# First stage of an encoder block: modulation weights transposed and summed along rows by VectorE, x transposed tile by tile, six column groups of w_in

## The chip, the cores and the metric

The kernel runs on one core of one Trainium2 chip. The metric is the device time of one execution in microseconds. The engines are TensorE (PE, and PEld for its weight loads), VectorE (DVE), ScalarE (ACT), GpSimd (POOL) and SyncE (SP), which issues nearly all DMA transfers here.

## What is computed

One layer of a transformer encoder on 512 tokens of width 2048, in float32. Only the parts around the change are kept here.

```python
c_act = silu(c)                                   # c: 1 x 2048
mod = c_act @ w_ada + b_ada                       # w_ada: 2048 x 12288
sh1, sc1, g1, sh2, sc2, g2 = split(mod, 6)        # 2048 values each
h = rms_norm(x, norm1_w) * (1 + sc1) + sh1        # x: 512 x 2048
proj = h @ w_in                                   # w_in: 2048 x 8704
qa, ka, va, qb, kb, vb, ga, gb = split(proj)      # 1024 256 256 1024 1024 1024 2048 2048
ya = global_attention(rope(norm(qa)), rope(norm(ka)), va)    # 8 heads, 2 k/v heads
yb = neighbourhood_attention(qb, kb, vb, bias)               # 8 heads
m = sigmoid(ga) * (ya @ w_oa) + sigmoid(gb) * (yb @ w_ob)
x = x + g1 * (m @ w_out)
h2 = rms_norm(x, norm2_w) * (1 + sc2) + sh2
x = x + g2 * ((silu(h2 @ w_gate) * (h2 @ w_up)) @ w_down)
out = rms_norm(x, final_w)
```

## The kernel before

Everything is tiled by 128: 16 k-tiles of the width (`KT`), four token tiles (`NT`). A matrix product is done in three matmuls (`mm3`, lines 122 to 124): each operand is split into a high part `hi`, a copy rounded to float32r by ScalarE (line 114), and a low part `lo`, the remainder, by VectorE or, where `eng=G` or `G` is given, GpSimd (line 115). `unit` loads a piece of a weight, at most 128x1024 (512 KB), into a `raw` buffer (4 of them), and `wsplit` splits it into `whi` and `wlo` (3 of each). `form2` makes 512 columns for all tokens (8 units of 24 matmuls of 128x512), `form1` 256 columns, transposed (4 units of 24). The first column groups of w_in are KA (256 columns of k and 256 of v), QA (first half of qA), QA + 512 (second half), VB and VB + 512 (halves of vB) and GA (gate columns 0 to 511).

The author's code states an order; a scheduler of the framework fixes at build time which instruction each engine and each DMA queue runs when, and where they wait. It goes by program order (`tc.high_priority()` puts a block ahead), by the readiness of inputs and by free buffers, so work of a later stage can be moved up to where an engine would be idle. On the chip each engine and each queue runs its list in that fixed order.

*First stage* (lines 299 to 396). x is loaded as 16 tiles of 128x512; squares and statistics give the row factor, line 325 scales the tiles, TensorE transposes all of them (line 328) and ScalarE copies them to `xnT`, which holds the whole of x transposed. For the shift and the scale of each k-tile `ada1` calls `ada_mod`: pieces of w_ada are loaded (line 242; rows of 512 bytes for one k-tile, 1 KB for two), VectorE multiplies each piece by its value of silu(c) and adds it to `acc` (lines 255 and 257), so that each of 16 parts leaves one partial sum per partition; TensorE sums over the partitions by matmuls with a column of ones (line 275), and lines 263 to 265 make `s` and `t`. The loop runs over nine slices (k-tile 0, k-tile 1, then pairs). In each, ScalarE makes `hf` from xnT (line 351) and the split gives h of that k-tile, with GpSimd for the low part; all w_in splits of the stage have GpSimd too. KA is summed in four banks over the whole stage (lines 359 to 364); QA and GA are done in batches of one to four k-tiles in other banks and added up in SBUF by VectorE (line 391). At the end GA goes to DRAM.

*Attention A.* k and q are normalised and rotated, four heads run, then `form2(w_in, QA + 512, ...)`, the gates of columns 512 to 1023, four more heads, the gates of columns 1024 to 2047.

*Attention B.* `bg` holds generators of background work; `pump`, called after each unit of `form1` and `form2`, advances the first of them by one step. Before attention B eight `ada_mod` for the second modulation (pairs of k-tiles, nine steps each) are put there. Each half of B makes v by `form2(w_in, VB + half * 512, ...)`, then q and k of two heads at a time by `form1` (32 units in all for both halves), then those heads. Then come the eight `ada_gate` (nine steps each) and the gates `sg_b` (32 units). Output projections and the feed-forward part follow; the change doesn't touch them.

Of the kernel before, what the change touches and what calls it, by code (L numbers as in the profile page):

```python
# [17 lines left out]
P = 128  # L18
D = 2048
# [61 lines left out]
def encoder_block(ctx: ExitStack, tc, xp, c, w_ada, b_ada, norm1_w, w_in, q_norm_w, k_norm_w, tb,  # L81
# [147 lines left out]
    t2 = const.tile([P, KT], F32, name="t2")  # L229

    accp = io

    def ada_units(cols, w, pool=None):

        nj = len(cols)
        nk = 1024 // (nj * w)
        for k0 in range(0, KT, nk):
            raw = (pool or wp).tile([P, 1024], F32, tag="raw", name="raw", bufs=5 if pool else wbufs["raw"])
            r4 = raw.rearrange("p (k c n) -> p k c n", k=nk, c=nj)
            for j, col in enumerate(cols):  # L240
                src = w_ada[k0 * P:(k0 + nk) * P, col:col + w]
                nc.sync.dma_start(r4[:, :, j], src.rearrange("(k p) n -> p k n", p=P))
            yield [(k0 + e, raw[:, e * nj * w:(e + 1) * nj * w]) for e in range(nk)]

    def ada_acc(cols, w, bias, pool=None):


        acc = accp.tile([P, 512], F32, tag="acc", name="acc", bufs=2)[:, :len(cols) * w]
        if bias:
            G.memset(acc, 0.0)  # L250
            nc.sync.dma_start(acc[0:1, :], b_ada[:, cols[0]:cols[0] + w])
        for parts in ada_units(cols, w, pool):
            for k, part in parts:
                if k == 0 and not bias:
                    V.tensor_scalar(acc, part, cact[:, k:k + 1], None, op0=ALU.mult)
                else:
                    V.scalar_tensor_tensor(acc, part, cact[:, k:k + 1], acc, op0=ALU.mult, op1=ALU.add)  # L257
            yield None
        yield acc

    def ada_done(y, k0, n, s, b_s, nw, t, b_t):
        sl = slice(k0, k0 + n)
        V.tensor_add(s[:, sl], y[:, :n], b_s[:, sl])
        V.tensor_add(t[:, sl], y[:, n:2 * n], b_t[:, sl])
        V.scalar_tensor_tensor(s[:, sl], s[:, sl], 1.0, nw[:, sl], op0=ALU.add, op1=ALU.mult)

    def ada_mod(sh, sc, k0, n, to, pool=None):

        for acc in ada_acc((sc + k0 * P, sh + k0 * P), n * P, False, pool):
            if acc is None:  # L270
                yield
        with tc.high_priority():
            y = bank("Y")
            for j in range(2 * n):
                nc.tensor.matmul(y[:, j:j + 1], acc[:, j * P:(j + 1) * P], ones[:, 0:1], start=True, stop=True)
            ada_done(y, k0, n, *to)
        yield

    def ada_gate(col, q, dst):

        for acc in ada_acc((col + q * 512,), 512, True):
            if acc is None:
                yield
# [8 lines left out]
        yield  # L292

    def rows(dst, src):
        for q in range(4):
            nc.sync.dma_start(dst[:, q * 512:(q + 1) * 512], src[q].partition_broadcast(P).rearrange("p o d -> p (o d)"))
# [3 lines left out]
    xt = [[p_h.tile([P, 512], F32, tag=f"h{15 - 2 * i - q // 2}{'hl'[q % 2]}", name=f"xt{i}{q}") for q in range(4)]  # L300
          for i in range(NT)]
# [5 lines left out]
    g_acc = [p_x.tile([P, T], F32, name=f"g_acc{j}") for j in range(4)]  # L307
# [22 lines left out]
    hT = [pair(p_h, f"h{k}", T, 1) for k in range(KT)]  # L330

    sg_a = [dram.tile([P, T], F32, name=f"sga{j}") for j in range(KT)]
    sg_b = [dram.tile([P, T], F32, name=f"sgb{j}") for j in range(KT)]
    kv_b = [bank("mm") for _ in range(NT)]
    turn = itertools.cycle("SST")
    slices = [(0, 1), (1, 2)] + [(k, k + 2) for k in range(2, KT, 2)]

    def ada1(k0, k1):  # L340
        to = (s1, b_sc1, n1, t1, b_sh1)
        for _ in ada_mod(0, D, k0, k1 - k0, to, p_x):
            pass

    ada1(*slices[0])
    for n, (k0, k1) in enumerate(slices):
        hp = tc.high_priority()
        hp.__enter__()
        for k in range(k0, k1):
            hf = io.tile([P, T], F32, tag="io", name="hf")  # L350
            S.activation(hf, xnT[:, k], AF.Identity, scale=s1[:, k:k + 1], bias=t1[:, k:k + 1])
            split(*hT[k], hf, G)
        hp.__exit__(None, None, None)
        ks = range(k0, k1)
        hi, lo = wsplit(w_in, k0, len(ks), KA, 512, G)
        for k in ks:
            for i in range(NT):
                sl = slice(i * P, (i + 1) * P)
                nc.tensor.matmul(kv_b[i], hT[k][0][:, sl], hi[:, k - k0], start=k == 0, stop=False)
                nc.tensor.matmul(kv_b[i], hT[k][0][:, sl], lo[:, k - k0], start=False, stop=False)  # L360
        for k in ks:
            for i in range(NT):
                sl = slice(i * P, (i + 1) * P)
                nc.tensor.matmul(kv_b[i], hT[k][1][:, sl], hi[:, k - k0], start=False, stop=k == KT - 1)
        if k1 == KT:
            kv = []
# [3 lines left out]
        for c0, accs, ends in ((QA, q_acc, (0, 1, 2, 4, 8, 12, 16)), (GA, g_acc, (0, 2, 6, 10, 14, 16))):  # L370
            if k1 not in ends:
                continue
            a0 = ends[ends.index(k1) - 1]
            ws = {}
            for k in range(a0, k1, 2):
                m = min(2, k1 - k)
                hi, lo = wsplit(w_in, k, m, c0, 512, G)
                ws.update({k + e: (hi[:, e], lo[:, e]) for e in range(m)})
            for i, acc in enumerate(accs):
                sl = slice(i * P, (i + 1) * P)  # L380
                b = bank(next(turn))
                for k in range(a0, k1):
                    (wh, wl), (hh, hl) = ws[k], hT[k]
                    if accs is q_acc:
                        mm3(b, hh[:, sl], hl[:, sl], wh, wl, k == a0, k == k1 - 1)
                    else:
                        mm3(b, wh[:, sl], wl[:, sl], hh, hl, k == a0, k == k1 - 1)
                if a0 == 0:
                    S.activation(acc, b, AF.Copy)
                else:  # L390
                    V.tensor_add(acc, acc, b)
        if n + 1 < len(slices):
            ada1(*slices[n + 1])
    for j in range(4):
        nc.sync.dma_start(sg_a[j], g_acc[j])
# [112 lines left out]
    form2(w_in, QA + 512, hT, lambda i, b: S.activation(q1[i], b, AF.Copy), eng=G)  # L508
# [72 lines left out]
    bg.extend(ada_gate(2 * D, q, g1_d) for q in range(4))  # L581
    bg.extend(ada_gate(5 * D, q, g2_d) for q in range(4))
# [378 lines left out]
```

## Time and profile before

| | us |
|---|---|
| median of three runs | 2812.9 |
| lowest and highest run | 2806.91, 2821.86 |
| span of the profiled execution | 2800.4 |
| TensorE busy | 2672.3 (95%) |
| VectorE busy | 1730.4 (62%) |
| ScalarE busy | 961.7 (34%) |
| GpSimd busy | 617.0 (22%) |

The span is the time from the first to the last instruction of one execution under the profiler; it is what the profile gives of that execution, and the runs' times include what lies around it. Matmuls are pipelined and their ends are modelled: a row of 0.39 us that is followed by the next after 0.23 us overlaps with it, so the starts tell the rate. The granted clock is the part of TensorE's full clock (2.4 GHz) that it was given, as a mean over the stretch. The name of a tile stands as output<-inputs, and for matmuls the moving operand comes first.

### The profile page before, as it was taken

What the parts mean: (1) busy time and instruction counts of PE and PEld (TensorE: products, weight loads), DVE (VectorE), ACT (ScalarE), POOL (GpSimd) and SP (SyncE); (2) the same over time, 40 slices, a digit from 0 to 9 for tenths busy, and PEclk for the clock granted to TensorE, in tenths of its full rate; (3) what the DMA queues carried; (4) which work ended last, traced back from release to release, by engine and by line L of the source; (5) the groups of instructions that cost most, each with busy time, mean ns of one, the idle gap of its engine ahead of it and who ended that gap; (6) DMA issues with size and microseconds to landing.
All of it is one profiled execution on the core that took longest, in us unless ns stands there. A gap on an engine that the chain in (4) does not pass through costs nothing.

```text
span 2800.4 us, 38853 instructions
## 1 busy us (share of the span) xinstructions
PE 2672.3 (95%) x15353; PEld 2331.3 (83%) x15353; DVE 1730.4 (62%) x2277; ACT 961.7 (34%) x1310; POOL 617.0 (22%) x366
## 2 busy tenths in 40 slices
PE   5888999999999999899899999999999989999998
PEld 4676878788887878677789999999999988878886
DVE  8987461566665566565568877777788753243227
ACT  4224441233331233222544444444444433122122
POOL 2544323000100000011123443333434410011000
PEclk8889999999999999999989999999999999999999
DMA  8772224655556577676333343334333354343232
GB/s 256 255 235 83 83 68 153 193 157 168 173 168 198 186 254 249 221 260 199 95 113 121 122 128 118 116 108 130 126 119 120 125 192 163 97 143 120 90 113 83
DMA packets 281238, 427.17 MB, mean 153 GB/s; under 512 B 16992, under 2 KB 148432, under 8 KB 278496
## 3 DMA queue, kind: packets, MB, share of 16 engines
q1 hardware_dynamic: 280720, 423.59, 46.9%
q8 instruction: 120, 1.97, 0.3%
q10 hardware_dynamic: 336, 1.11, 0.1%
q14 instruction: 62, 0.51, 0.1%
HBM read 392.11 MB, written 32.52 MB: 152 GB/s over the span
## 4 chain that ended last, share of the span: by engine, by line
PE 77%; DVE 10%; DMA 8%; ACT 2%; issue 2%; SPq 0%; POOL 0%; DVEq 0%; ACTq 0%
PE mm L122 19%; PE mm L124 19%; PE mm L123 19%; DMA raw<-in_w_ada 6%; DVE acc L257 5%; PE S L122 3%; PE S L123 3%; PE S L124 3%; PE Y L122 2%; PE Y L123 2%; PE Y L124 2%; DMA ffr<-ffd 1%; ACT whi L114 1%; PE T L494 1%; DVE wlo L115 0%
## 5 line engine op out<-in xcount | busy, mean ns | idle before, releaser
L114 ACT ACTIVATE whi<-raw 128x1024 fp32r<-128x1024 f32 (+1 forms) x466 | 455.2, 978 | 1077.0 <-PE mm L124 404.8
L115 DVE TENSOR_TENSOR wlo<-raw,whi 128x1024 fp32r<-128x1024 f32 (+1 forms) x408 | 499.4, 1227 | 494.6 <-ACT whi L114 489.7
L257 DVE SCALAR_TENSOR_TENSOR acc<-raw,cact,acc 128x512 f32<-128x512 f32 (+1 forms) x383 | 324.9, 851 | 138.0 <-DMA raw<-in_w_ada 129.0
L707 POOL TENSOR_TENSOR tb<-raw 128x512 f32<-128x512 f32 x84 | 116.0, 1380 | 505.6 <-DVE wlo L115 497.8
L115 POOL TENSOR_TENSOR wlo<-raw,whi 128x1024 fp32r<-128x1024 f32 (+1 forms) x58 | 142.7, 2465 | 236.5 <-ACT whi L114 204.9
L115 DVE TENSOR_TENSOR wlo<-ta,whi 128x1024 fp32r<-128x1024 f32 x84 | 129.4, 1541 | 70.5 <-ACT whi L114 70.1
L708 POOL TENSOR_TENSOR tb<-ta,raw 128x512 f32<-128x512 f32 x84 | 145.1, 1727 | 0.0
L646 POOL TENSOR_TENSOR xr<-xr,ro 128x512 f32<-128x512 f32 x32 | 49.3, 1572 | 434.0 <-DVE ro L645 434.0
L114 ACT ACTIVATE whi<-ta 128x1024 fp32r<-128x1024 f32 x84 | 89.2, 1062 | 142.1 <-PE mm L123 142.1
L114 ACT ACTIVATE whi<-tb 128x1024 fp32r<-128x1024 f32 x84 | 89.1, 1061 | 133.4 <-PE S L123 119.9
L123 PE MATMUL mm<-x1l,whi 128*128 128x256 f32 x400 | 112.4, 281 | 0.0
L122 PE MATMUL mm<-x1h,whi 128*128 128x256 f32 x400 | 112.3, 281 | 0.0
L124 PE MATMUL mm<-x1h,wlo 128*128 128x256 f32 x400 | 112.3, 281 | 0.0
L115 DVE TENSOR_TENSOR wlo<-tb,whi 128x1024 fp32r<-128x1024 f32 x84 | 102.5, 1221 | 10.0 <-ACT whi L114 8.3
L122 PE MATMUL mm<-x0h,whi 128*128 128x256 f32 x368 | 104.5, 285 | 3.3 <-ACT whi L114 3.3
L124 PE MATMUL mm<-x0h,wlo 128*128 128x256 f32 x368 | 104.4, 284 | 0.8 <-DVE wlo L115 0.8
L123 PE MATMUL mm<-x0l,whi 128*128 128x256 f32 x368 | 104.5, 284 | 0.0
L250 POOL MEMSET acc<- 128x512 f32 x8 | 4.2, 526 | 427.9 <-DVE ada_s L115 158.6
L123 PE MATMUL mm<-x3l,whi 128*128 128x256 f32 x336 | 94.3, 281 | 0.0
L123 PE MATMUL S<-x2l,whi 128*128 128x256 f32 x336 | 94.3, 281 | 0.0
L123 PE MATMUL S<-x3l,whi 128*128 128x256 f32 x336 | 94.3, 281 | 0.0
L123 PE MATMUL mm<-x2l,whi 128*128 128x256 f32 x336 | 94.3, 281 | 0.0
(1311 smaller groups left out, 8242.9 us busy)
## 6 DMA issues: line engine op xcount, KB each, us to landing
raw<-in_w_in SPq DMA_DIRECT2D x134, 512.0 KB
raw<-in_w_ada SPq DMA_DIRECT2D x256, 256.0 KB
raw<-in_w_gate SPq DMA_DIRECT2D x88, 512.0 KB
raw<-in_w_up SPq DMA_DIRECT2D x88, 512.0 KB
raw<-in_w_down SPq DMA_DIRECT2D x88, 512.0 KB
raw<-in_w_ada SPq DMA_DIRECT2D x64, 512.0 KB
raw<-in_w_out SPq DMA_DIRECT2D x40, 512.0 KB
ffr<-ffd SPq DMA_DIRECT2D x22, 512.0 KB
```

The lines of the kernel that those rows point to most:

```text
L114: S.activation(hi, src, AF.Copy)
L115: eng.tensor_sub(lo, src, hi)
L122: nc.tensor.matmul(o, lh, rh, start=start, stop=False, **kw)
L123: nc.tensor.matmul(o, lh, rl, start=False, stop=False, **kw)
L124: nc.tensor.matmul(o, ll, rh, start=False, stop=stop, **kw)
L250: G.memset(acc, 0.0)
L257: V.scalar_tensor_tensor(acc, part, cact[:, k:k + 1], acc, op0=ALU.mult, op1=ALU.add)
L494: nc.tensor.transpose(tp[:, k * P:(k + 1) * P], e[:, k * P:(k + 1) * P], ident)
L646: eng.tensor_add(x2[i][:, cs], x2[i][:, cs], o)
L707: G.tensor_sub(t3, b22, b12)
L708: G.tensor_sub(t4, t2_, b21)
```

## The change

The modulation weights are laid out anew outside the kernel: `w_mod` is sh1, sc1, sh2, sc2 transposed (8192 rows of 2048), `w_gmod` the two gate parts side by side. c is broadcast to all 128 partitions and its SiLU taken there (`c_rows`). The shift and the scale of a k-tile are now sums along rows: four instructions on VectorE, each over 128x1024, multiply a piece by `cb` and give the sum as a second output; no matmul with ones is needed, and the sum is already one value per partition. In the first stage this is done two k-tiles ahead; in attention B it is background work of 16 generators with two steps each.

xnT is gone: `h_tile` transposes x for one k-tile when it is needed. Six column groups instead of three are made in the first stage: the second half of qA and both halves of vB join, are added up in SBUF in batches of four k-tiles (as GA is now, in place of its old ends), stored to DRAM, and loaded again where the later `form2` made them. All splits of the stage go to VectorE. The ada_gate reads w_gmod in the same pieces as before.

```diff
+    for b_s in (b_sc1, b_sc2):
+        V.tensor_scalar(b_s, b_s, 1.0, None, op0=ALU.add)
...
+    def c_rows(pool):
+        cb = pool.tile([P, D], F32, name="cb")
+        nc.scalar.dma_start(cb, c.partition_broadcast(P).rearrange("p o d -> p (o d)"))
+        S.activation(cb, cb, AF.Silu)
+        return cb
+
+    def ada_mod(m, k, cb, to, pool, tag, bufs):
+        s, b_s, nw, t, b_t = to
+        y = small.tile([P, 2, 2], F32, tag="mod", name="mod")
+        for j in range(2):
+            r0 = (2 * m + 1 - j) * D + k * P
+            for e in range(2):
+                es = slice(e * 1024, (e + 1) * 1024)
+                raw = pool.tile([P, 1024], F32, tag=tag, name="araw", bufs=bufs)
+                nc.sync.dma_start(raw, w_mod[r0:r0 + P, es])
+                V.scalar_tensor_tensor(raw, raw, 1.0, cb[:, es], op0=ALU.mult, op1=ALU.mult,
+                                       accum_out=y[:, e, j:j + 1])
+            if j == 0:
+                yield
+        with tc.high_priority():
+            z = small.tile([P, 2], F32, tag="modz", name="modz")
+            V.tensor_add(z, y[:, 0], y[:, 1])
+            V.scalar_tensor_tensor(s[:, k:k + 1], z[:, 0:1], b_s[:, k:k + 1], nw[:, k:k + 1], op0=ALU.add, op1=ALU.mult)
+            V.tensor_add(t[:, k:k + 1], z[:, 1:2], b_t[:, k:k + 1])
+        yield
...
-    xnT = p_x.tile([P, KT, T], F32, name="xnT")
-            tp = bank("S")
-            for j in range(4):
-                nc.tensor.transpose(tp[:, j * P:(j + 1) * P], xt[i][q][:, j * P:(j + 1) * P], ident)
-            S.activation(xnT[:, 4 * q:4 * q + 4, i * P:(i + 1) * P], tp.rearrange("p (k t) -> p k t", k=4), AF.Copy)
...
+    keep = {QA + 512: q1_d, VB: vb_d[0], VB + 512: vb_d[1], GA: sg_a[:4]}
+    accs = {QA: q_acc} | {c0: [p_x.tile([P, T], F32, name=f"acc{c0}_{j}") for j in range(4)] for c0 in keep}
+    EARLY, LATE = (0, 1, 2, 4, 8, 12, 16), (0, 4, 8, 12, 16)
...
+    def ada1(k):
+        for _ in ada_mod(0, k, cb, (s1, b_sc1, n1, t1, b_sh1), p_x, "araw", 4):
             pass
+    def h_tile(k):
+        with tc.high_priority():
+            tp = bank("Y")
+            for i in range(NT):
+                nc.tensor.transpose(tp[:, i * P:(i + 1) * P], xt[i][k // 4][:, k % 4 * P:(k % 4 + 1) * P], ident)
             hf = io.tile([P, T], F32, tag="io", name="hf")
+            S.activation(hf, tp, AF.Identity, scale=s1[:, k:k + 1], bias=t1[:, k:k + 1])
+            hT.append(pair(p_h, f"h{k}", T, 1))
+            split(*hT[k], hf)
+    ada1(0)
+    ada1(1)
+    for k in range(KT):
+        h_tile(k)
+        if k % 2 == 0:
+            whi, wlo = wsplit(w_in, k, 2, KA, 512)
+        for i in range(NT):
+            sl = slice(i * P, (i + 1) * P)
+            mm3(kv_b[i], hT[k][0][:, sl], hT[k][1][:, sl], whi[:, k % 2], wlo[:, k % 2], k == 0, k == KT - 1)
...
+        for c0, acc in accs.items():
+            ends = EARLY if c0 == QA else LATE
+            if k + 1 not in ends:
                 continue
+            a0 = ends[ends.index(k + 1) - 1]
             ws = {}
+            for k0 in range(a0, k + 1, 2):
+                m = min(2, k + 1 - k0)
+                hi, lo = wsplit(w_in, k0, m, c0, 512)
+                ws.update({k0 + e: (hi[:, e], lo[:, e]) for e in range(m)})
...
                 if a0 == 0:
+                    S.activation(acc[i], b, AF.Copy)
                 else:
+                    V.tensor_add(acc[i], acc[i], b)
+                if k == KT - 1 and c0 in keep:
+                    nc.sync.dma_start(keep[c0][i], acc[i])
+        if k + 2 < KT:
+            ada1(k + 2)
...
-    form2(w_in, QA + 512, hT, lambda i, b: S.activation(q1[i], b, AF.Copy), eng=G)
+    for i in range(NT):
+        nc.sync.dma_start(q1[i], q1_d[i])
...
-    bg.extend(ada_mod(3 * D, 4 * D, k, 2, (s2, b_sc2, n2, t2, b_sh2)) for k in range(0, KT, 2))
+    cb = c_rows(p_b)
+    bg.extend(ada_mod(1, k, cb, (s2, b_sc2, n2, t2, b_sh2), wp, "raw", 4) for k in range(KT))
     for half in range(2):
         v = [pair(p_b, "v", 512, NT) for _ in range(NT)]
-        form2(w_in, VB + half * 512, hT, lambda i, b: split(*v[i], b))
+        for i in range(NT):
+            vr = wp.tile([P, 1024], F32, tag="raw", name="vr", bufs=4)[:, :512]
+            nc.sync.dma_start(vr, vb_d[half][i])
+            split(*v[i], vr)
```

## Rows read from the trace of the kernel before

**Rows 1.** The page: span, engines (busy us, share, instructions).

```profile
span 2800.4 us, 38853 instructions
...
PE 2672.3 (95%) x15353; PEld 2331.3 (83%) x15353; DVE 1730.4 (62%) x2277; ACT 961.7 (34%) x1310; POOL 617.0 (22%) x366
```

**Rows 2.** Stretches: length, busy us by engine, granted clock, DMA share, GB/s.

```profile
0.00:40.00 40.00, 15.84 (x69) 12.60 (x69) 29.72 (x100) 23.18 (x46) 5.14 (x9) 0.87 0.80 251
40.00:226.50 186.50, 161.07 (x636) 128.76 (x637) 155.71 (x186) 58.05 (x118) 90.71 (x41) 0.87 0.72 233
500.00:800.00 300.00, 297.07 (x1398) 244.53 (x1397) 180.88 (x327) 91.30 (x154) 20.16 (x21) 1.00 0.54 169
800.00:980.00 180.00, 177.22 (x795) 145.72 (x794) 97.05 (x147) 43.34 (x60) 0.53 (x1) 0.98 0.60 187
```

**Rows 3.** TensorE in order of time, 222 to 232 us (start, us, instruction).

```profile
222.46 0.39 PE L122 MATMUL T<-h14h,whi 128*128 128x512 f32 x1
...
226.54 0.39 PE L122 MATMUL mm<-whi,h0h 128*128 128x512 f32 x1
...
231.98 0.39 PE L122 MATMUL mm<-whi,h2h 128*128 128x512 f32 x1
```

**Rows 4.** TensorE in order of time, 36 to 75 us.

```profile
40.35 0.79 PE L359 MATMUL mm<-whi,h0h 128*128 128x512 f32 x1 [2.42 <-ACT h0h L114]
...
70.73 0.63 PE L359 MATMUL mm<-whi,h2h 128*128 128x512 f32 x1
...
72.86 0.63 PE L360 MATMUL mm<-wlo,h2h 128*128 128x512 f32 x1
```

**Rows 5.** Groups by shape, 0 to 226.5 us (busy us, mean ns, idle).

```profile
L257 DVE SCALAR_TENSOR_TENSOR acc<-raw,cact,acc 128x512 f32<-128x512 f32 x105 | 121.0, 1153 | 2.9
L115 POOL TENSOR_TENSOR wlo<-raw,whi 128x1024 fp32r<-128x1024 f32 x24 | 64.2, 2684 | 63.2 <-ACT whi L114 58.3 <-issue 4.7
L114 ACT ACTIVATE whi<-raw 128x1024 fp32r<-128x1024 f32 x24 | 25.2, 1055 | 72.5 <-DMA raw<-in_w_in 67.4 <-PE T L124 2.0 <-PE S L124 1.5
L257 DVE SCALAR_TENSOR_TENSOR acc<-raw,cact,acc 128x256 f32<-128x256 f32 x30 | 15.7, 546 | 0.3
L328 PE MATMUL S<-ident,xt 128*128 128x128 f32 x64 | 14.4, 413 | 14.0 <-DVE xt L325 14.0
...
L391 DVE TENSOR_TENSOR st<-st,S 128x512 f32<-128x512 f32 x14 | 9.5, 686 | 14.4 <-PE S L124 14.4
...
L420 ACT ACTIVATION_READ_ACCUMULATOR junk<-st 128x1 f32 x24 | 4.7, 195 | 0.0
```

**Rows 6.** Groups by shape, 500 to 800 us.

```profile
L257 DVE SCALAR_TENSOR_TENSOR acc<-raw,cact,acc 128x512 f32<-128x512 f32 x79 | 60.5, 766 | 31.6 <-DMA raw<-in_w_ada 30.5
L115 DVE TENSOR_TENSOR wlo<-raw,whi 128x1024 fp32r<-128x1024 f32 x47 | 59.1, 1257 | 55.5 <-ACT whi L114 55.2 <-DMA raw<-in_w_ada 0.3
```

**Rows 7.** Waits, 0 to 226.5 us (us in total, times, longest us).

```profile
ACT hf L351 <- DVE s L265: 36.2, 8, 6.7
PE Y L275 <- DVE acc L257: 21.2, 8, 4.0
```

**Rows 8.** VectorE in order of time, 18 to 33.5 us.

```profile
21.50 0.48 DVE L257 SCALAR_TENSOR_TENSOR acc<-raw,cact,acc 128x256 f32<-128x256 f32 x1
...
30.98 1.66 DVE L325 TENSOR_SCALAR xt<-xt,rr 128x512 f32<-128x512 f32 x4
```

**Rows 9.** Line 257, 500 to 800 us (ns min/median/max, first and last start).

```profile
L257 DVE SCALAR_TENSOR_TENSOR acc<-raw,cact,acc x79: 733/752/1359, 501.5 to 798.4; 128x512 f32<-128x512 f32 x79
```

**Rows 10.** Chain that ended last, 500 to 560 us.

```profile
504.09 2.98 DMA raw<-in_w_ada
...
514.18 1.02 PE Y L275 x8
...
525.71 4.38 DMA raw<-in_w_ada
```

**Rows 11.** Chain that ended last, 222 to 262 us (start, us, what).

```profile
228.25 5.22 DMA sga<-g_acc
```

More of the change, by code (lines that the diff above doesn't have):

```diff
@@ L80, in encoder_block @@
 @with_exitstack
-def encoder_block(ctx: ExitStack, tc, xp, c, w_ada, b_ada, norm1_w, w_in, q_norm_w, k_norm_w, tb,
+def encoder_block(ctx: ExitStack, tc, xp, c, w_mod, w_gmod, b_ada, norm1_w, w_in, q_norm_w, k_norm_w, tb,
                   w_oa, w_ob, w_out, norm2_w, w_gate, w_up, w_down, final_w, rope, wmask, out):
@@ L245, in ada_acc @@
[L245 to L283, printed above, removed]
+    def ada_gate(g, q, dst):
+        acc = accp.tile([P, 512], F32, tag="acc", name="acc", bufs=2)
+        G.memset(acc, 0.0)
+        col = (2 + 3 * g) * D + q * 512
+        nc.sync.dma_start(acc[0:1, :], b_ada[:, col:col + 512])
+        for k0 in range(0, KT, 2):
+            _, r3 = unit(w_gmod, k0, 2, g * D + q * 512, 512)
+            for e in range(2):
+                V.scalar_tensor_tensor(acc, r3[:, e], cact[:, k0 + e:k0 + e + 1], acc, op0=ALU.mult, op1=ALU.add)
+            yield
@@ L292, in ada_gate @@
         yield
+    def c_rows(pool):
[8 more added lines that the diff above has]
+            r0 = (2 * m + 1 - j) * D + k * P
+            for e in range(2):
+                es = slice(e * 1024, (e + 1) * 1024)
[10 more added lines that the diff above has]
+            V.tensor_add(t[:, k:k + 1], z[:, 1:2], b_t[:, k:k + 1])
+        yield
     def rows(dst, src):
@@ L306, in encoder_block @@
     p_x = tc.alloc_tile_pool(name="p_x", bufs=1, side="right")
-    g_acc = [p_x.tile([P, T], F32, name=f"g_acc{j}") for j in range(4)]
-    xnT = p_x.tile([P, KT, T], F32, name="xnT")
+    xplace = {(i, q): f"h{8 + 2 * q + i // 2}{'hl'[i % 2]}" for i in range(NT) for q in range(3)}
+    xt = [[p_h.tile([P, 512], F32, tag=xplace[i, q], name=f"xt{i}{q}") if q < 3 else
+           p_x.tile([P, 512], F32, name=f"xt{i}{q}") for q in range(4)] for i in range(NT)]
+    cb = c_rows(p_x)
     for i in range(NT):
@@ L325, in encoder_block @@
             V.tensor_scalar(xt[i][q], xt[i][q], r, None, op0=ALU.mult)
-            tp = bank("S")
-            for j in range(4):
-                nc.tensor.transpose(tp[:, j * P:(j + 1) * P], xt[i][q][:, j * P:(j + 1) * P], ident)
-            S.activation(xnT[:, 4 * q:4 * q + 4, i * P:(i + 1) * P], tp.rearrange("p (k t) -> p k t", k=4), AF.Copy)
-    hT = [pair(p_h, f"h{k}", T, 1) for k in range(KT)]
+    hT = []
     sg_a = [dram.tile([P, T], F32, name=f"sga{j}") for j in range(KT)]
     sg_b = [dram.tile([P, T], F32, name=f"sgb{j}") for j in range(KT)]
+    q1_d = [dram.tile([P, T], F32, name=f"q1d{i}") for i in range(NT)]
@@ L336, in encoder_block @@
+    vb_d = [[dram.tile([P, T], F32, name=f"vbd{h}{i}") for i in range(NT)] for h in range(2)]
+    keep = {QA + 512: q1_d, VB: vb_d[0], VB + 512: vb_d[1], GA: sg_a[:4]}
+    accs = {QA: q_acc} | {c0: [p_x.tile([P, T], F32, name=f"acc{c0}_{j}") for j in range(4)] for c0 in keep}
+    EARLY, LATE = (0, 1, 2, 4, 8, 12, 16), (0, 4, 8, 12, 16)
     kv_b = [bank("mm") for _ in range(NT)]
     turn = itertools.cycle("SST")
[L338 to L342, printed above, removed]
-            pass
@@ L345, in encoder_block @@
[L345 to L349, printed above, removed]
-            hf = io.tile([P, T], F32, tag="io", name="hf")
[L351 to L366, printed above, removed]
+    def ada1(k):
+        for _ in ada_mod(0, k, cb, (s1, b_sc1, n1, t1, b_sh1), p_x, "araw", 4):
+            pass
@@ L579, in encoder_block @@
                 att_b(h0 + j, qk[j], qk[2 + j], v, slice((hp * 2 + j) * HD, (hp * 2 + j + 1) * HD))
-    bg.extend(ada_gate(2 * D, q, g1_d) for q in range(4))
-    bg.extend(ada_gate(5 * D, q, g2_d) for q in range(4))
+    bg.extend(ada_gate(0, q, g1_d) for q in range(4))
+    bg.extend(ada_gate(1, q, g2_d) for q in range(4))
     gates(sg_b, GB, 0, KT)
@@ L945 @@
     tb = tb.reshape(nh * ROWS, TB_LEN)
+    sh1, sc1, gm1, sh2, sc2, gm2 = np.split(np.asarray(w_ada[0]), 6, axis=1)
     arrays = {
-        "xp": token_order(np.asarray(x)[0]), "c": f(c), "w_ada": f(w_ada[0]), "b_ada": f(b_ada),
+        "xp": token_order(np.asarray(x)[0]), "c": f(c), "w_mod": f(np.concatenate([m.T for m in (sh1, sc1, sh2, sc2)])), "w_gmod": f(np.concatenate([gm1, gm2], axis=1)),
+        "b_ada": f(b_ada),
         "norm1_w": f(norm1_w), "w_in": f(w_in[0]), "q_norm_w": f(q_norm_w), "k_norm_w": f(k_norm_w), "tb": tb,
```

39 lines of the change are left out of this document (8 added, 31 removed).

## Prediction

> **What bounds the kernel now.** I read the page first [rows 1]: TensorE is busy 95% of a span of 2800.4 us, so only stretches in which it is idle or slowly clocked can give time back. Of the profiled execution only that span is given; the median of the runs, 2812.9, lies 12.5 us above it. I work in differences and add them to the median.
>
> The table of stretches [rows 2] shows where such a stretch lies: the first stage. Up to 226.5 us TensorE is busy 176.9 us at a granted clock of 0.87; from 500 to 800 it is busy 297 of 300 at 1.00. How much of the first stage was needed? At full clock (2.4 GHz) the matmuls of 128x512 follow each other every 0.2267 us: 43 rows from 222.46 to 231.98, 9.52/42 [rows 3]. At half clock (1.2 GHz) it is 0.426 us: 70.73 to 72.86 in five steps [rows 4]. Three column groups are 3 x 16 x 4 x 3 = 576 matmuls, 131 us at full clock. The next stage's first matmul (into mm from h0h) starts at 226.54 [rows 3]. So some 95 us of the first stage are not its matmuls.
>
> VectorE holds it. It is busy 185.4 of the 226.5 us [rows 2], 136.7 of them in line 257, the weighted sum over the modulation weights. Over 512 columns that takes 1153 ns on average here [rows 5] and 766 ns later, with little on GpSimd [rows 6]; in the first stage GpSimd splits weights at 2684 ns each [rows 5]. The waits close the argument [rows 7]: TensorE's ones-matmuls wait for those sums (21.2 us), and ScalarE's h tile waits for the scale from VectorE, 36.2 us in 8 waits. The transfers, at a share of 0.72 and 233 GB/s [rows 2], are not what holds the stage.
>
> **The change, part by part.**
>
> *TensorE.* Six groups are 1152 matmuls, 261 us at 0.2267. Three of them come from later (the second half of qA, both halves of vB), where TensorE already ran at nearly full rate: 576 x 0.2267 = 131 us go there. The work is the same in sum; the point is whether stage one fills up. Its ends compare as: old 226.5 + 131 = 357 us against the new end.
>
> *VectorE, first stage.* The new sums are 16 x 4 = 64 over 1024 columns. The trace has no VectorE instruction that also accumulates. Line 257 takes 0.48 us at 256 columns [rows 8] and 0.752 (median) at 512 [rows 9]; the same slope gives 1.30 at 1024. Reading out an accumulator costs ScalarE 195 ns [rows 5]; I take 1.30 + 0.17 = 1.47. Lower bound: the subtraction over 1024 columns, 1.26 [rows 6]; upper bound: two passes, 2.6. Sum: 64 x 1.47 = 94 us, and three small ones per k-tile, an estimated 7 in all. Splits come over from GpSimd: 48 units x 1.26 = 60 us, 16 h tiles x 0.69 = 11. Additions into the accumulators: 20 + 4 x 12 = 68 instead of 36, at 0.686 [rows 5], 22 more. From 185 I take 137 (line 257) and an estimated 9 (its first products and small sums) and add 94 + 7 + 60 + 11 + 22: 233 us. That is below TensorE's 261, so TensorE becomes the bound, and the disturbance by GpSimd is gone.
>
> *DMA.* 33.5 MB modulation, 25.2 w_in, 4.2 x, 1.0 for the broadcast c: 64 MB. 233 GB/s at a share of 0.72 is 324 at full share [rows 2]: 198 us, hidden under TensorE; uncovered, before h3, it counts below. The SiLU of c costs two 1024-column activations at 1.06 [rows 5], about 2 us, under the load of x.
>
> *Start.* Before, the last rows of x are scaled at 30.98 [rows 8] and the first h matmul starts at 40.35 [rows 4]. That order stays; the transposes move behind the scaling. I put the first matmul at 38 (36 to 42). Four of the six groups cannot start until h3 is there: x, c, four modulation tiles and w_in for k 0 to 3 are 15.7 MB, 63 us at the first stretch's 251 GB/s [rows 2], 48 at 324; VectorE has about 50 us of work. I take 57. TensorE has 60 matmuls in hand until then. From 57 on: 1092 x 0.2267 = 248 us, plus 48 transposes; before, 64 of them are 14.4 us of busy time [rows 5], overlapped; I take 8. That makes 313 without any stall.
>
> *Stalls.* Each batch (k = 3, 7, 11, 15) is five groups back to back with two weight units each, on three weight buffers. The second unit of a group can be split only when the group before is nearly through: 1.06 us ScalarE plus 1.26 VectorE against 6 matmuls (1.4 us) in hand, up to 18 if three banks are opened at once. 16 such boundaries x 1 us = 16 us (0 to 40). Half clock in the thin work before h3: 60 x 0.2 = 12 at most; I take 7. New end 313 + 16 + 7 = 336: **-21 us** (-44 to +10).
>
> *Removed ones-matmuls.* In stage one they are within the above. For the second modulation 8 groups of 8 take 1.02 us each [rows 10] on a busy TensorE: **-8 us**.
>
> *Transition.* After stage one the chain goes through the store of the last accumulators, 5.22 us [rows 11], then the rotary work; that remains. The squares for k and q now run during the last batch: **-3 us** (0 to -5). The reload of q1 and v lies under the gate and q/k projections; without that cover each is one landing, 3 to 4 us [rows 10]. The gates of columns 4 to 8 take over from the removed qA projection as filler of the transition, equally long (192 matmuls, 43.5 us).
>
> *Second modulation.* It has 32 steps in place of 72, two 512 KB transfers each, and the vB projections that carried 16 of the steps are gone: all of it falls in the 32 q/k units. From 500 to 800 VectorE is busy 180.9 us, 60.5 of them in line 257 [rows 2, 6]. Without these, the small sums and 16 vB splits (20 us) some 96 remain; 64 x 1.47 + 7 makes 197, against TensorE's 297 - 87 - 4 = 206. So VectorE goes from 60% to 96% there, in order, with weight splits queued behind sums that wait for a transfer, and TensorE waits for those splits. Attention heads can slip into the sb gates behind, where VectorE has 83 of 180 us free [rows 2]. I take **+10 us** (0 to +30). The DMA is costed at nothing: 1.5 MB per unit of 24 matmuls (5.4 us) are 4.6 us at 324 GB/s.
>
> Sum: -21 - 8 - 3 + 10 = **-22 us**, so 2791, a span of about 2778.
>
> **A rule that speaks against it.** Line 257 has two f32 inputs in SBUF and runs at (0.752 - 0.48)/256, 1.06 ns per column, without accumulating [rows 8, 9]. The Trainium skill ("Vector Engine (DVE) Microarchitecture Reference", section 7, Points that are easy to get wrong) says that this instruction with two non-bf16 SBUF sources has its throughput halved, because both read ports are taken and none is left for reading back the accumulator. No run so far shows the accumulating form. By that rule the sum would be the half-rate rival's, 2845.
>
> **Rivals.**
> *Half rate (the other side).* If the accumulating form takes two passes, 2.5 us, VectorE has 66 us more in stage one, 299: per four k-tiles about 73 us against TensorE's 67, which puts the end some 20 later. In the q/k stretch it needs 265 us against 206; less what slips behind, +43 in place of +10. Sum 2791 + 20 + 33 = about 2845. It decides once the instruction takes over 2.0 us. For it: two streams and an accumulator; against: line 257's slope. Chance 0.13.
> *The q/k stretch starves.* Four raw buffers serve three transfers per unit. With landings of 3 to 4.4 us [rows 10] a unit needs about (4 + 2.3 + 2 x 5.5)/4 = 4.3 us, below 5.4; with landings of 7 us it is 6.6, and 32 x 1.2 = 38 us are lost in place of 10: about 2819. Chance 0.12.
> *Stage one does not fill.* If the fixed order on VectorE puts sums ahead of splits, boundary stalls are 2 us and h3 comes at 65: the end is 336 + 16 + 8 = 360, -21 becomes +3, and the time 2815. For it: ScalarE's waits for the scale in the old stage [rows 7], with the splits queued behind; against: their source, the disturbed sums, is gone. Chance 0.20.
> *Forecast:* 0.55, its own range 2766 to 2804.
>
> **How the numbers follow.** 0.5% of this time, 14 us, is about what a measurement can tell from no change. Faster than 2799: nine tenths of the forecast (0.50), the mild ends of the unfilled stage (0.04) and of starving (0.02): 0.56. Slower than 2827: half rate 0.12, starving 0.05, unfilled 0.01: 0.18. The rest, 0.26, is the same. The range 2762 to 2832 takes in the bounds of the stalls and of starving, and leaves out most of half rate and a stage with no stall at all.
>
> **What would show it.** Right: the last group of stage one ends near 336 with the granted clock at 1.00 from some 60 us on; the sums take 1.4 to 1.5 us; GpSimd is idle until then; the ones-matmuls are gone. Wrong: sums over 2.0 us; TensorE waiting at group boundaries for wlo; TensorE idle in the q/k stretch while VectorE waits for w_mod; h3 after 65 us.

## The result

The changed kernel takes 2816.1 us (median of 20 runs, 2804.5 to 2821.8), the kernel before in the same series 2810.0 (20 runs, 2803.2 to 2821.9): ratio 1.0019, interval 1.0010 to 1.0027. The forecast was 2791 (2762 to 2832), some 22 us faster; the first stage gave more than it said, and attention B took all of it back.

The page after, its first line and that of TensorE:

```profile
span 2816.3 us, 38449 instructions
...
PE 2660.6 (94%) x15225; PEld 2314.6 (82%) x15225; DVE 1715.7 (61%) x2389; ACT 967.1 (34%) x1304; POOL 503.0 (18%) x316
```

The spans differ by 15.9 us [rows 1], the medians by 6.1. A run's time lies 1.8 us over its span (after: 2818.1 and 2816.3), so the profiled execution of before is some 8 us under its median and that of after 2 us over it. The accounts below are made between the two profiles, and the verdicts between the medians; some 10 us of the accounts are the choice of these two executions.

**The first stage.** The start of the next stage in TensorE's timeline (it answers to the last rows of [rows 3]):

```profile
321.55 0.39 PE L124 MATMUL S<-h15h,wlo 128*128 128x512 f32 x1
321.77 0.39 PE L122 MATMUL mm<-h0h,whi 128*128 128x512 f32 x1
```

It comes at 321.77 instead of 226.54, 95.2 us later, with 576 x 0.2267 = 130.6 us of matmuls more behind it: -35.4 us. The sums, in the groups by shape of VectorE from 0 to 330 us:

```profile
L273 DVE SCALAR_TENSOR_TENSOR araw<-araw,cb 128x1024 f32<-128x1024 f32 x64 | 77.2, 1218 | 17.7 <-DMA araw<-in_w_mod 17.6
L115 DVE TENSOR_TENSOR wlo<-raw,whi 128x1024 fp32r<-128x1024 f32 x47 | 57.2, 1221 | 37.4 <-ACT whi L114 37.4
...
L273 DVE DVE_READ_ACCUMULATOR araw<-araw,cb 128x1 f32 x64 | 5.2, 81 | 0.0
```

A sum over 1024 columns takes 1218 ns, no more than the subtraction below it, and 81 ns for the read-out of the accumulator.

**Attention B.** The table of stretches after; columns as in [rows 2]:

```profile
40.00:330.00 290.00, 281.44 (x1241) 228.09 (x1241) 181.59 (x303) 96.02 (x157) 7.62 (x4) 1.00 0.63 209
...
560.00:640.00 80.00, 73.51 (x331) 59.49 (x330) 60.92 (x127) 25.25 (x44) 3.21 (x3) 0.96 0.72 234
640.00:690.00 50.00, 39.54 (x151) 29.97 (x150) 27.08 (x67) 14.93 (x34) 5.39 (x6) 0.76 0.34 109
...
740.00:760.00 20.00, 12.05 (x38) 8.69 (x39) 10.62 (x29) 6.15 (x14) 2.30 (x3) 0.61 0.56 182
...
810.00:820.00 10.00, 3.48 (x17) 2.85 (x17) 2.02 (x6) 1.73 (x3) 2.30 (x3) 0.80 0.47 156
...
552.00:834.00 282.00, 248.28 (x1073) 196.84 (x1073) 191.89 (x415) 83.93 (x158) 17.97 (x21) 0.90 0.61 198
560.00:840.00 280.00, 246.28 (x1064) 195.21 (x1063) 191.39 (x410) 84.14 (x158) 17.97 (x21) 0.90 0.61 198
```

The first stage is now full, 281 of 290 us at a granted clock of 1.00. Attention B and the sb gates behind it run from the end of the last `sga<-go` store (551.98) to that of the last `sgb<-go` store (1005.09): 453.1 us. Before, from 494.06 to 994.38, they took 500.3; without the 384 moved vB matmuls (87.1) and the ones-matmuls (8) 405.2 should be left. **47.9 us are lost there**, in a few places: 580 to 600, 640 to 690, 740 to 760 and 810 to 820, with TensorE idle or at a low clock. Before, TensorE was busy 297 of 300 us in this part at 1.00 [rows 2]. The whole account of the two profiles: first stage -35.4; transition and attention A +6.2 (551.98 - 321.77 = 230.2, against 267.5 - 43.5 for the moved qA); ones-matmuls -8; attention B and its gates +47.9; all behind them +5.2 (in the kernels below, e9 apart, this part of the profile differs by as much, 1805 to 1812 us, for the same work): +15.9.

Who waits there? The waits after, 545 to 840 us, with the total, the number and the longest:

```profile
POOL bm L524 <- DMA braw<-in_tb: 163.3, 5, 71.9
ACT whi L114 <- DMA raw<-in_w_in: 84.4, 21, 7.0
...
DVE araw L273 <- DMA araw<-in_w_mod: 29.8, 25, 3.1
...
PE S L122 <- DVE sb L540: 14.6, 5, 6.5
...
SPq L453 <- ACT yo L452: 44.8, 7, 18.3
SPq L272 <- DVE wlo L115: 40.0, 19, 4.7
SPq L272 <- DVE araw L273: 39.1, 26, 3.9
```

Weight splits wait for w_in 84 us, and a DMA queue itself waits: SyncE's stands 44.8 us at line 453, the store of a finished head, and 79 us at line 272, a w_mod load for which VectorE has yet to free a buffer. Waits of the second kind were there before too, 69 us at the w_ada loads from 494 to 820. Three pieces of the timeline after show three places, in order of time; rows between them are left out:

```profile
586.72 0.38 SPq L129 DMA_DIRECT2D raw<-in_w_in  x1
587.86 1.47 SPq L272 DMA_DIRECT2D araw<-in_w_mod  x2
590.14 0.38 SPq L129 DMA_DIRECT2D raw<-in_w_in  x1
591.99 1.06 ACT L114 ACTIVATE whi<-raw 128x1024 fp32r<-128x1024 f32 x1 [7.04 <-DMA raw<-in_w_in]
...
640.29 1.95 SPq L564 DMA_DIRECT2D vr<-vbd  x4
644.09 5.38 SPq L519 DMA_DIRECT2D braw<-in_tb  x16
667.87 0.35 SPq L453 DMA_DIRECT2D y<-yo  x1
...
675.83 0.63 ACT L114 ACTIVATE vh<-vr 128x512 fp32r<-128x512 f32 x1
677.22 0.40 SPq L129 DMA_DIRECT2D raw<-in_w_in  x1
...
742.65 0.60 ACT L452 ACTIVATE yo<-Y 128x512 f32<-128x512 f32 x1 [1.88 <-PE Y L124]
743.28 0.35 SPq L453 DMA_DIRECT2D y<-yo  x1
743.67 1.00 SPq L519 DMA_DIRECT2D braw<-in_tb  x3
745.22 0.40 SPq L129 DMA_DIRECT2D raw<-in_w_in  x1
746.53 2.30 POOL L524 TENSOR_TENSOR bm<-braw,msk 128x384 f32<-128x384 f32 x3 [18.75 <-DMA braw<-in_tb]
748.21 0.89 DVE L540 SCALAR_TENSOR_TENSOR sb<-S,bm 128x256 f32<-128x256 f32 x2 [6.98 <-POOL bm L524]
748.69 0.69 PE L122 MATMUL S<-qkh 128*128 128x384 f32 x1 [6.07 <-DVE sb L540]
```

1. Two w_mod transfers stand between one w_in load and the next, on buffers that VectorE must free; the split waits 7 us.
2. At 640 the four transfers of the second half's vB (`vr`) take all four raw buffers. They are split only from 675.83 on, when the heads of the first half let go of `v`; so no w_in load goes out between 629.73 and 677.22, and TensorE has nothing but heads. In the same gap, after 16 bias transfers, the queue stands at a store of `y` until 667.87, the longest of the seven waits (18.3 us): two holders lie over each other here.
3. At 743 the queue has stood at the store of head output `y`, which waits for ScalarE's copy. Behind it are the last three of the 16 transfers of the next head's bias, and w_in. GpSimd, VectorE and TensorE wait one after the other, TensorE 6.07 us.

Which of the three matters, or whether a full VectorE does, was for experiments.

### The profile page after: what moved, and what is told of

Same layout as the page of the kernel before. It is cut to its first block, busy times and chain, and to the rows that moved or that the text cites. A ratio compares the mean times of both kernels' runs of the same rounds, so it can differ in the third digit from the quotient of the medians.

```text
span 2816.3 us, 38449 instructions
## 1 busy us (share of the span) xinstructions
PE 2660.6 (94%) x15225; PEld 2314.6 (82%) x15225; DVE 1715.7 (61%) x2389; ACT 967.1 (34%) x1304; POOL 503.0 (18%) x316
## 4 chain that ended last, share of the span: by engine, by line
PE 52%; DVE 1%; DMA 1%; ACT 1%; issue 1%; POOL 0%; DVEq 0%; ACTq 0%
PE mm L124 13%; PE mm L122 13%; PE mm L123 13%; PE S L123 3%; PE S L122 3%; PE S L124 3%; PE Y L123 1%; PE Y L122 1%; PE Y L124 1%; DMA ffr<-ffd 1%; PE T L783 0%; ACT eo L784 0%; DVE ro L638 0%; DVE wlo L115 0%; PE S L783 0%
## 5 line engine op out<-in xcount | busy, mean ns | idle before, releaser
L115 DVE TENSOR_TENSOR wlo<-raw,whi 128x1024 fp32r<-128x1024 f32 (+1 forms) x441 | 536.7, 1220 | 527.2 <-ACT whi L114 525.6
L114 ACT ACTIVATE whi<-raw 128x1024 fp32r<-128x1024 f32 x465 | 455.6, 980 | 1040.1 <-PE mm L124 365.8
L273 DVE SCALAR_TENSOR_TENSOR araw<-araw,cb 128x1024 f32<-128x1024 f32 x128 | 154.9, 1220 | 54.7 <-DMA araw<-in_w_mod 54.4
L244 DVE SCALAR_TENSOR_TENSOR acc<-raw,cact,acc 128x512 f32<-128x512 f32 x128 | 96.0, 750 | 97.2 <-DMA raw<-in_w_gmod 95.0
L115 POOL TENSOR_TENSOR wlo<-raw,whi 128x1024 fp32r<-128x1024 f32 x24 | 57.9, 2414 | 425.7 <-ACT whi L114 382.0
L115 DVE TENSOR_TENSOR wlo<-tb,whi 128x1024 fp32r<-128x1024 f32 x84 | 102.6, 1221 | 9.6 <-ACT whi L114 7.8
```

The source lines that it names most:

```text
L114: S.activation(hi, src, AF.Copy)
L115: eng.tensor_sub(lo, src, hi)
L244: V.scalar_tensor_tensor(acc, r3[:, e], cact[:, k0 + e:k0 + e + 1], acc, op0=ALU.mult, op1=ALU.add)
L273: V.scalar_tensor_tensor(raw, raw, 1.0, cb[:, es], op0=ALU.mult, op1=ALU.mult, accum_out=y[:, e, j:j + 1])
```

## The experiments

All twelve kernels were timed in five rounds, each group (e1 to e4; e5, e6, e8 and e9; e10 to e13) beside the kernel before, so kernels of different groups are compared by their ratios. `vr` is the reload of vB, "spread" means one w_mod transfer per background step in place of two. "B and gates" is the time from the end of the last `sga<-go` store to that of the last `sgb<-go` store in the profile, "lost" is what it has over 405.2 (over 492.3 where vB is projected inside).

| kernel | us | ratio to before, interval | B and gates | lost |
|---|---|---|---|---|
| changed | 2816.1 | 1.0019 (1.0010 to 1.0027) | 453.1 | 47.9 |
| e1: vr apart | 2807.1 | 0.9992 (0.9982 to 1.0002) | 448.8 | 43.5 |
| e2: y stores apart | 2804.8 | 0.9986 (0.9975 to 0.9996) | 443.6 | 38.4 |
| e3: vr, y | 2788.9 | 0.9927 (0.9912 to 0.9942) | 430.1 | 24.9 |
| e10: spread | 2789.9 | 0.9938 (0.9919 to 0.9958) | 429.1 | 23.9 |
| e11: vr, spread | 2781.1 | 0.9901 (0.9880 to 0.9923) | 427.7 | 22.5 |
| e12: y, spread | 2788.5 | 0.9939 (0.9917 to 0.9960) | 429.2 | 24.0 |
| e5: vr, y, spread | 2767.6 | 0.9861 (0.9841 to 0.9880) | 411.6 | 6.4 |
| e4: sums short | 2806.0 | 0.9990 (0.9977 to 1.0003) | 449.6 | 44.4 |
| e6: vr, y, sums short | 2777.0 | 0.9898 (0.9881 to 0.9916) | 416.8 | 11.6 |
| e8: vB in B | 2769.6 | 0.9875 (0.9853 to 0.9898) | 504.1 | 11.8 |
| e13: vB in B, y, spread | 2775.1 | 0.9888 (0.9868 to 0.9907) | 502.7 | 10.4 |
| e9: vr, y, gates between | 2803.7 | 0.9993 (0.9980 to 1.0005) | | |

**e1: vr in buffers of its own.**

```
-            vr = wp.tile([P, 1024], F32, tag="raw", name="vr", bufs=4)[:, :512]
+            vr = p_b.tile([P, 512], F32, tag="vr", name="vr", bufs=4)
```

> The reload of vB gets four buffers of its own in attention B instead of the four raw buffers that the weights use. Theory 'held buffers': after the change the second reload holds all four raw buffers from 640 to 677 us, until the first half's heads give v free; the stretch from 650 to 690, where TensorE loses some 10 us idle and 9 at half clock, closes, and the kernel is 12 to 20 us faster than the changed kernel (about 2798). Rival 'VectorE is full': the sums of the second modulation set the pace there, buffers are not it: less than 5 us. Rival 'transfers': two w_mod transfers per unit set the pace: less than 5 us.

**e2: the y stores of attention B on ScalarE's queue.**

```
-        nc.sync.dma_start(y_d[h], o)
+        (nc.sync if h < 8 else nc.scalar).dma_start(y_d[h], o)
```

> The eight stores of the attention outputs of B are issued from ScalarE's queue instead of SyncE's. Theory 'queue order': on SyncE's queue a store that waits for its head stands ahead of the bias loads of the next head and of the weights (743 and 813 us in the changed kernel); the gaps of 6 us each with the slow clock after them go, 15 to 22 us (about 2798), and GpSimd's bias no longer waits for braw past the store. Rivals 'VectorE is full' and 'transfers': less than 5 us, the gaps stay in another place.

**e3: both edits.**

> Both edits. If the two losses are separate they add up: 27 to 40 us against the changed kernel, about 2782, and faster than the kernel before by 1%. If they are one loss seen at two places (the stretch has too little filler or VectorE is full), the second edit brings little on top of the first: 2795 to 2810.

Against the changed kernel e1 gives 0.27% and e2 0.33%, 8 and 9 us, above the rivals' 5 and well short of the two theories (12 to 20 and 15 to 22); both together give 0.92%, 26 us, just under the 27 to 40 of separate losses. Of what e1 gains in its profile, 12.5 us, 7.3 lie ahead of attention B and only 4.3 in it and its gates. Alone, each is worth little in B because the other holder is there next. SyncE's timeline of e1, the whole of 645 to 665 us, where the loads could now go on:

```profile
660.55 0.35 SPq L453 DMA_DIRECT2D y<-yo  x1
661.00 0.87 SPq L272 DMA_DIRECT2D araw<-in_w_mod  x2
661.96 0.38 SPq L129 DMA_DIRECT2D raw<-in_w_in  x1
662.44 5.00 SPq L272 DMA_DIRECT2D araw<-in_w_mod  x2
```

Nothing is issued from 645 to 660.55, and then the store of y goes first: with vr out of the way the queue stands at the store. The table of stretches of e1 in the same place:

```profile
660.00:670.00 10.00, 1.43 (x8) 0.79 0.83 284
```

TensorE is busy 1.43 of 10 us (here the columns are TensorE, clock, DMA share and GB/s). In e2 it is the other way round, on SyncE's queue:

```profile
636.80 4.89 SPq L564 DMA_DIRECT2D vr<-vbd  x4
...
675.21 0.40 SPq L129 DMA_DIRECT2D raw<-in_w_in  x1
```

No w_in load goes out between them, with the store gone from the queue.

**e4: the second modulation's sums over 64 of 1024 columns.**

```
+                n = 1024 if m == 0 else 64
+                V.scalar_tensor_tensor(raw[:, :n], raw[:, :n], 1.0, cb[:, ...], ..., accum_out=y[:, e, j:j + 1])
```

> The sums of the second modulation run over 64 columns instead of 1024 (most of that modulation is left out, and the output with it); all loads stay. This takes about 74 us from VectorE in the q/k stretch. Theory 'VectorE is full': the loss in B goes, 30 us or more, about 2780. Theories 'held buffers' and 'queue order': the stretch keeps its gaps, under 12 us gained.

**e6: the same with both edits of e3.**

> As the kernel with both edits, but the second modulation's sums run over 64 of 1024 columns (all loads stay; most of the second modulation's arithmetic is left out), so VectorE loses about 70 us of work around attention B. Theory (VectorE has room once stores and raw buffers are out of the way): 2781 to 2789, no more than 8 us below 2788.9. Rival (VectorE, full in order, holds the rest): 2769 or less.

The stretch of e4 that answers to the last row of the stretches after:

```profile
560.00:840.00 280.00, 247.91 (x1097) 198.57 (x1097) 140.36 (x416) 84.76 (x159) 16.19 (x21) 0.92 0.62 204
```

VectorE does 51 us less here, TensorE only 1.6 us more; the whole time is 0.29% under that of the changed kernel, 8 us. A full VectorE does not explain the loss as long as the other holders stand. In e6 more comes back: 8 us by the ratios (0.29% under e3, on 0.9898 and 0.9927, intervals that just overlap), 13.3 us of attention B and its gates by the profiles. The time, 2777.0, lies between the theory's range and the rival's: once the queue is freer, the length of VectorE's sums counts. That it does so by freeing raw buffers sooner is argued and not shown; e4, made with the other holders in place, could not show it.

**e5: e3 and the second modulation spread, one transfer per background step from the fourth k-tile on (56 steps in place of 32, into the sb gates).**

```
-            if j == 0:
-                yield
+                if (j, e) == (0, 1) or (m == 1 and k >= 4 and (j, e) != (1, 1)):
+                    yield
```

> As the kernel with both edits (2788.9), but from the fourth k-tile on each background step of the second modulation issues one 512 KB transfer and its sum instead of two, so that 56 steps instead of 32 reach on into the sb gates. Theory (what is left of attention B's loss is whi waiting for w_in behind two w_mod transfers per unit, 76.9 us in 19 waits): 2774 to 2781, and those waits halved. Rival (the rest is attention work with nothing to fill TensorE, not the transfers): within 4 us of 2789.

0.66% under e3, 18 us, more than the 8 to 15 expected. Attention B in e5's table of stretches, the whole and two places of the gaps:

```profile
580.00:600.00 20.00, 16.37 (x82) 13.30 (x81) 15.74 (x42) 8.54 (x17) 0.00 (x0) 1.00 0.73 234
650.00:690.00 40.00, 39.99 (x193) 32.71 (x192) 31.76 (x69) 16.39 (x31) 4.40 (x5) 1.00 0.60 191
...
545.00:779.00 234.00, 227.36 (x1082) 185.10 (x1081) 159.44 (x351) 84.78 (x159) 18.63 (x21) 1.00 0.57 182
```

and in its waits, 545 to 840:

```profile
ACT whi L114 <- PE mm L123: 76.2, 20, 4.4
...
ACT whi L114 <- DMA raw<-in_w_in: 31.9, 11, 6.5
```

The waits for w_in are less than half (31.9, after 84.4, in e3 76.9). ScalarE's splits now wait mostly for TensorE to free a weight buffer, as they should where TensorE sets the pace. TensorE is busy 227.36 us at a clock of 1.00 for about as many matmuls (1082) as took 248.28 at 0.90 after (1073): of the 48 us by which that stretch is longer after (282 against 234), some 21 were slower matmuls in and behind the gaps, the rest the gaps themselves. What moved on into the gates costs something there: from the last head store to the last gate store are 175.0 to 176.8 us in the four kernels that are the changed one with the spread, 169.1 to 172.2 in the changed kernel and in e1 to e4 and e6. The spread moves the sums along with their transfers, and e6 shows that the sums count too; no run parts the two, so of the 18 us only the whole is shown.

**e10 to e12: the spread alone, and with one of the other two.**

> The changed kernel with the spread alone (one transfer of the second modulation per step from the fourth k-tile on; vr stays in the raw buffers, the y stores on SyncE's queue). Theory (three causes, each with its own wait; none is worth much alone): 2800 to 2810. Rival (two transfers per step were the whole cause, the other two only followed from it): 2785 or less.

> The changed kernel with vr in buffers of its own and the spread; the y stores stay on SyncE's queue ahead of the loads. Theory (the stores still hold back the next head's bias and w_in, 6 to 7 us at each of two or three places): 2782 to 2795. Rival (with a transfer less per step the loads run far enough ahead): 2772 or less, as with all three edits.

> The changed kernel with the y stores on ScalarE's queue and the spread; vr stays in the four raw buffers. Theory (vr holds them over a pair of heads, TensorE short by some 12 to 15 us near the middle of attention B): 2778 to 2790. Rival (not needed): 2772 or less.

The spread alone is worth 0.81%, 23 us, more than I thought and less than its rival. It is the largest single part, and the other two do not follow from it: e12 still has the gap of vr. Stretches of e12, with the columns of e1's:

```profile
650.00:660.00 10.00, 6.16 (x33) 0.99 0.01 2
660.00:670.00 10.00, 6.78 (x24) 0.50 0.08 29
670.00:680.00 10.00, 6.65 (x19) 0.50 0.66 209
```

Nearly nothing moves on the DMA engines from 650 to 670, and the clock is 0.50 for 20 us. e12 ended inside its theory's range, at the upper end, e11 just under it. With the spread done and vr in the way, freeing the stores gives nothing (e10 and e12: 0.9938, 0.9939); when the other two are done, the stores give 0.40%, the spread 0.66% and vr 0.78%. Only all three together bring the lost time to 6.4 us.

**e8: vB projected in attention B again, four column groups in the first stage.**

```
-    keep = {QA + 512: q1_d, VB: vb_d[0], VB + 512: vb_d[1], GA: sg_a[:4]}
+    keep = {QA + 512: q1_d, GA: sg_a[:4]}
...
-            vr = wp.tile([P, 1024], F32, tag="raw", name="vr", bufs=4)[:, :512]
-            nc.sync.dma_start(vr, vb_d[half][i])
-            split(*v[i], vr)
+        form2(w_in, VB + half * 512, hT, lambda i, b: split(*v[i], b))
```

> As the changed kernel, but vB is projected in attention B again, as before; stage one has four column groups (kA, both halves of qA, the first gates). Theory (attention B lost its filler and the raw buffers to the reload of vB): stage one ends near 250, attention B takes about 325 us with TensorE busy above 97% of it, last attention output stored near 803, time 2790 to 2800. Rival (the second modulation's new form costs attention B its 45 us wherever vB is made): last attention output stored near 840, time 2830 or more.

With vB left where it was, the change is 1.25% faster than before. The first stage ends at 229.60, 3.1 us after the old one with 43.5 us of matmuls more, so -40.4; the two vB groups of the changed kernel bring nothing more there (-35.4). I had put this end at 250, which is most of why the time came below 2790. Attention B and its gates still lose 11.8 us, the clearest gaps in the first third. This kernel has no reload of vB, and a third of its 48 units are vB's projections, so it changes two things at once: what holds the buffers, and what TensorE has in hand. How the gain divides between them is not shown. The last attention output is stored at 799.11, 342 us after attention A and not 325, but the scheduler had moved gates ahead of it, so that this mark misleads; the end of the gates is the better one. Rows of e8's stretches in that third, with the columns of e1's:

```profile
500.00:510.00 10.00, 3.34 (x10) 0.72 0.61 192
...
550.00:560.00 10.00, 4.42 (x20) 0.95 0.82 267
```

**e13: e8 with the y stores and the spread.**

> The kernel with vB projected in attention B (2769.6) and also the y stores on ScalarE's queue and the spread. Theory (the 18 us by which its attention B still exceeds that of before, 342.7 against 325, are the same waits for w_mod ahead of w_in): 2752 to 2761, attention B at most 330. Rival (the vB projections already cover them): 2766 to 2773.

The theory fell, and the time lies 2 us above the rival's range too: attention B and its gates take 502.7 us, in e8 504.1. That is not because nothing was left to gain. The gap of e8 at 550 to 560 is closed (TensorE busy 10.00 of 10 us for 4.42), and the last head store comes 334.3 us after attention A for 342.1; but the gates behind it take 168.4 us for 162.0, so most of it is lost again there (about ten matmuls, some 2 us of either difference, only changed sides). The two intervals overlap; the 5 us by which the median is above that of e8 stand in its profile behind the gates (1811.5 us against 1806.3), where the kernels do the same.

**e9: e3 with the sb gates between the heads, four columns behind each k projection.**

```
+    bg.extend(ada_gate(0, q, g1_d) for q in range(4))
+    bg.extend(ada_gate(1, q, g2_d) for q in range(4))
     for half in range(2):
...
+            gates(sg_b[h0 * 2:], GB + h0 * 2 * P, 0, 4)
...
-    bg.extend(ada_gate(0, q, g1_d) for q in range(4))
-    bg.extend(ada_gate(1, q, g2_d) for q in range(4))
-    gates(sg_b, GB, 0, KT)
```

> As the kernel with both edits, but the 16 sb gates are no longer all behind attention B: four of them stand behind each k projection, ahead of the heads of that pair, and the second modulation's gate rows follow its sums without a pause. Theory (heads without projections to fill TensorE lose the rest): last sb gate stored 10 to 20 us earlier than 975, time 2769 to 2779, granted clock at 1.00 through attention B. Rival (loads hold it): within 4 us of 2789, and whi's waits for w_in stay near 77 us.

0.66% above e3, 18 us, where 10 to 20 less were expected, and the rival had it within 4. The waits for w_in stayed, as the rival said; e9's waits from 545 to 825:

```profile
ACT whi L114 <- DMA raw<-in_w_in: 80.4, 16, 7.6
```

What was lost on top shows in e9's timeline, in order of time, where the last heads now end the stage in place of gates:

```profile
948.36 0.83 SPq L389 DMA_DIRECT2D sgb<-go  x2
...
972.31 11.07 SPq L590 DMA_DIRECT2D yr<-y  x12
...
989.60 0.77 PE L122 MATMUL mm<-y0h,whi 128*128 128x512 f32 x1 [19.20 <-ACT whi L114]
```

The last head output goes out at 971.07, and the next stage begins by reading the outputs back; TensorE is idle 19.20 us before its first matmul. In the order of the other kernels the gates lie over that. From attention A to this last store are 425 us, to the last gate store of e3 430.1, so the gates between the heads gave some 5 us: in this arrangement the heads' lack of filler is a small part (the gate rows' loads also moved ahead, and were not tried apart), and the order cost more than it gave.

## Why the prediction was wrong, step by step

- *First stage, -21.* Right in kind, too small: -35.4. The sum over 1024 columns costs 1.30 us with the read-out (1.47 estimated), and VectorE is busy 210 us up to 330 instead of the 233. The start is later than I put it (first matmul of h at 42.56 for 38, of h3 at 60.62 for 57), but the 16 us of stalls at group boundaries did not come: from 60.62 to 321.77 are 261 us, where 1092 matmuls and the transposes alone were put at 256.
- *The half-rate rival and the rule beside it.* Fallen: 1218 ns, where it needed over 2.0 us to decide. The trace does not agree with the rule of the Trainium skill ("Vector Engine (DVE) Microarchitecture Reference", section 7, Points that are easy to get wrong: throughput halved with two non-bf16 SBUF sources), as the prediction read it, a halving against the same form without accumulation (1.30 us by line 257's slope): this form has two f32 sources in SBUF and an accumulator, and takes as long as the plain subtraction (1221 ns).
- *"Stage one does not fill".* Fallen: clock 1.00, 281 of 290 us.
- *Ones-matmuls, -8.* Right: e5's busy time in B, 227.4, is that of before in B (322.1 from 494 to 819) less 87.1 and 8. *Transition, -3.* With attention A +6.2 instead, and the cause is open. This part is 224 to 227 us in five kernels where vr has its own buffers and 228 to 230 in four where it has not, but 230.9 in e6, which has them, and 227.3 in e4, which has not.
- *"The reload of q1 and v lies under the gate and q/k projections; without that cover each is one landing, 3 to 4 us."* One of the two steps that failed. I costed the transfer and not the buffers that it holds: vr sits in all four raw buffers from 640 until the heads let go of `v` at 676, and everything that needs a raw buffer stands behind it. Not one landing, but 47 us without a w_in load, part of them the store's (in e1, with vr apart, it is 26 us, from 635.84 to 661.96). With the other two repairs done, vr is worth 22 us (e12 to e5).
- *Second modulation, +10 (0 to +30), and "The DMA is costed at nothing".* The other failed step, and the mis-sized term of the sum: +47.9 for this and the reload together, outside its own range. The path was wrong as well: TensorE was to wait for splits queued behind sums on VectorE, and its waits for wlo are 5.0 us from 545 to 840, while the splits' waits for w_in are 84.4. I had the two transfers per unit and the four buffers in the "starves" rival, at 38 us with landings of 7, but gave it 0.12 and looked for the limit in VectorE (96%). VectorE is busy 68% there (191 of 280 us), and e4 shows that its work alone is not the limit; its sums count for 8 to 13 us once the queue is freer (e6). I counted bytes, and at a share of 0.61, and of 0.34 in the widest gap (640 to 690), these do not set the pace; what stands in the queue and holds its buffers does. Of the signs of being wrong that I named, one came in part: VectorE's sums wait 29.8 us for w_mod. The stores of y stood on that queue before as well, with smaller waits (26.4 us in 8 waits for ScalarE from 500 to 980, the longest 10.1, against 44.8 in 7, the longest 18.3, after). I never named what stands behind them.
- *vB's projections.* I counted their 16 units as carriers of background steps, and not as matmuls that TensorE has in hand while the queue is held: with them (e8) 11.8 us are lost, without them 47.9. Since e8 has no reload either, what they are worth alone is not shown.

The first stage's gain was there all along: e5, whose three repairs change no arithmetic, is 38 us under before, where the forecast had 22. What held it back were three holders of one queue, each of which hides the others; how far the spread works through the transfers and how far through VectorE's sums is open. That 2816.1 lies inside the stated range is luck: the first stage gave 14 us more than forecast, and attention B lost 38 us more.

## What to carry to other kernels

Where a step is moved and its result reloaded, cost the buffers that the reload holds and until when, not the transfer. Before adding loads to a queue write down its order, and name each entry that waits for an engine (a store of a result, a load into a shared buffer): everything behind it waits too. When two repairs alone give almost nothing, try them together before dropping either; here 8 and 9 us became 26, and 44 with the third. The same holds for an edit that is to exclude a cause: it excludes it only with the other holders in place (shorter sums, e4 and e6).

## What was not expected of the hardware

- A store that waits for its producer holds up all loads behind it on its queue: SyncE's queue stood 44.8 us in seven such waits in attention B, the longest 18.3. With the stores on ScalarE's queue (e3) this line is gone from SyncE's waits, though the profile puts two waits of SyncE's loads (9.5 and 8.4 us) down to the landing of a `y` store there. The Trainium skill ("Perfetto Trace Analysis", section DMA Optimizations) suggests one engine for inputs and another for outputs. What that gave here hangs on the other holders: 9 us alone (e2), 18 on top of e1 (e3), 11 on top of e11 (e5), nothing on top of e10 (e12).
- The gaps cost twice: in and behind them the granted clock fell, to 0.76 over 640 to 690 and 0.61 over 740 to 760, between half (1.2 GHz) and full clock (2.4 GHz), in e12 to half itself for 20 us; some 21 of the 48 us by which attention B is longer than in e5 are longer busy time for about as many matmuls.
- Reading VectorE's accumulator takes 81 ns, against 195 ns on ScalarE [rows 5].
